# v projected for four heads at a time instead of two, in 512-column matmuls over four PSUM banks

## The chip, the cores and the metric

The kernel runs on one core of a Trainium2 chip. The metric is device time in microseconds (us) of one execution, with all transfers from and to device memory in it. TensorE (PE) multiplies, VectorE (DVE), ScalarE (ACT) and GpSimd (POOL) do the rest, and SyncE (SP) and POOL issue the transfers.

## What is computed

One encoder block on 512 tokens of width 2048, in float32. Cut to what matters:

```python
h = rmsnorm(x, norm_mix_g)
dq, dk, dv, nq, nk, nv = split(h @ w_in, 6)          # each 512 x 1024, 8 heads of 128
# differential attention, 8 heads: two softmaxes per head over all 512 keys
a = softmax(q1 @ k1.T / 8) - lam * softmax(q2 @ k2.T / 8)     # q, k with partial rotary
a_out = rmsnorm(a @ dv, subln_g) * (1 - lambda_init)
# neighbourhood attention, 8 heads: each token sees 8 x 16 neighbours on the 8 x 64 grid
n_out = softmax(nq @ nk.T / sqrt(128) + rel_bias + mask) @ nv
x = x + concat(a_out, n_out) @ w_out
x = x + square(relu(rmsnorm(x, norm_mlp_g) @ w_up)) @ w_down
y = rmsnorm(x, norm_final_g)
```

The two v, dv and nv, are 512 tokens x 1024 columns each, contracted over 2048 rows of w_in.

## The kernel before

Products are made in three matmuls: each float32 operand is split into a high part (`wh`, by a cast on ACT) and a remainder (`wl`, by a subtraction on DVE, of every third unit in the attention part on POOL), and high x high, high x low and low x high are summed in PSUM (`mm3`, L97 to L100). A unit of weights is 128 x 1024 float32, 512 KB, loaded and split by `load_unit` (L72 to L91). In the host's layout, a unit of w_dv or w_nv holds four k-tiles of 128 rows by 256 columns, that is two heads; there are four units to such a block. A unit of q or k weights holds eight k-tiles of 128 columns, one head.

PSUM has eight banks of 512 float32 columns per partition. Pool psA (four banks, `psa()`) serves the projections and later w_out, psB and psC (two banks each) the attention.

`v_banks` (L129) takes two banks of psA and cuts each into two halves of 256 columns, so that each of the four row tiles t of 128 tokens has a half. `v_mm` (L133) runs the matmuls of one unit for one row tile: the stationary operand is hT (x transposed, times the norm's gain, split into two parts), the moving one the 256 columns of the weights. `v_out` (L144) scales a row tile by the row norm r, once on ACT for the high part and once on DVE for the remainder.

The start (L150 to L193): the v block of heads 0 and 1 (`pv0`) is accumulated while x arrives. For each of four groups of four k-tiles, one unit of weights and the x tiles are loaded on SP's queue; ACT writes the high part of hT (L165), DVE the remainder (L166), and PE runs `v_mm`. The squares of x go through ACT (L178) and are added up on POOL (L179), a last addition is DVE's (L180), and a matmul with ones sums over partitions (L183). From that `rstd_of` (L102 to L112) makes r on DVE and ACT, and only then can `v_out` scale pv0.

The attention part (L406 to L420) goes through pairs of heads: `proj_v` for dv (but for the first pair, whose dv is pv0), `diff_head` of the first head, `proj_v` for nv, `na_head` of the first head, `diff_head` and `na_head` of the second; in the last pair both `diff_head` come first. `diff_head` (L274) projects q and k (`proj_T`, 48 matmuls of 512 columns into one bank of psA, L232), rotates and stacks them, and per row tile makes scores (L291, L292), softmax (L293 to L299) and transposes (L303); then probabilities times v, and a norm. `na_head` (L335) does the like for the neighbourhood. The last four halves of heads go to `mixT` on chip, the earlier ones by way of device memory, and w_out (L500 on) follows.

The order of the instructions on each engine is written ahead by a planner that weighs priorities and its own estimates of durations; at run time each engine takes its instructions in that order and waits by semaphores. The start has the highest priority, unit loads of the attention part are advanced (`ahead=3000`), everything else goes by program order. A buffer of a pool (a PSUM bank, say) can be taken again only when all readers of its former content are done. `ones_f` (L126) is a tile of ones, copied into `ones_r` (L201) later; `lam4` and `lprod` (L124, L222) hold the four lambda vectors and their products; `tb` (L339) is the bias table of a neighbourhood head.

Of the kernel before, what the change touches and what calls it, by code (L numbers as in the profile page):

```python
# [9 lines left out]
F32 = mybir.dt.float32  # L10
F32R = mybir.dt.float32r
# [10 lines left out]
NH = 8  # L22
# [13 lines left out]
def hymba_kernel(ctx: ExitStack, tc: tile.TileContext, x, x_t, norm_mix_g, w_dq, w_dk, w_dv, w_nq, w_nk, w_nv, lams,  # L36
# [20 lines left out]
    def psa():  # L57
        return psA.tile([P, 512], F32, name="pa", tag="pa")
# [38 lines left out]
    def mm3(ps, lh, ll, rh, rl, first, last):  # L97
        nc.tensor.matmul(out=ps, lhsT=lh, rhs=rh, start=first, stop=False)  # L98
        nc.tensor.matmul(out=ps, lhsT=lh, rhs=rl, start=False, stop=False)  # L99
        nc.tensor.matmul(out=ps, lhsT=ll, rhs=rh, start=False, stop=last)  # L100
# [16 lines left out]
    def hT_k(kt, hl):  # L117
        return hT[kt // 4][:, hl, kt % 4, :]
# [4 lines left out]
    nc.scalar.dma_start(out=gT, in_=norm_mix_g)  # L123
    lam4 = ap0.tile([P, 4 * 64], F32, name="lam4")  # L124
    rB = ap0.tile([P, SEQ], F32, name="rB")
    ones_f = ap0.tile([P, P], F32, name="ones_f")  # L126
    nc.vector.memset(ones_f, 1.0)

    def v_banks():  # L129
        b = [psa() for _ in range(2)]  # L130
        return [b[t // 2][:, (t % 2) * 256:(t % 2 + 1) * 256] for t in range(NT)]

    def v_mm(ps, t, u, wh, wl):  # L133

        ts = slice(t * P, (t + 1) * P)
        for k in range(4):
            kt = 4 * u + k
            first, last = kt == 0 and t % 2 == 0, kt == NK - 1
            lh, ll = hT_k(kt, 0)[:, ts], hT_k(kt, 1)[:, ts]
            for i, (a, b) in enumerate(((lh, wh), (lh, wl), (ll, wh))):  # L140
                nc.tensor.matmul(out=ps[t], lhsT=a, rhs=b[:, k, :], start=first and i == 0, stop=last and i == 2,  # L141
                                 skip_group_check=True)

# [7 lines left out]
    with tc.tile_pool(name="start", bufs=4) as sp, tc.high_priority(offset=20000):  # L151
        acc = sp.tile([P, 2 * SEQ], F32, name="acc", bufs=1)
        xs = []
        for u in range(4):

            wh, wl = load_unit(w_dv[0, u], 256, pool=sp, ahead=0, cuts=2 if u == 0 else 1)
            xt = sp.tile([P, 4, SEQ], F32, name="xt", tag="xt")
            n = 4 if u == 0 else 2
            for i in range(n):
                ks = slice(i * 4 // n, (i + 1) * 4 // n)  # L160
                nc.sync.dma_start(out=xt[:, ks, :], in_=x_t[u].rearrange("p (k s) -> p k s", k=4)[:, ks, :])
            xs.append(xt)
            for k in range(4):
                g, hi = gT[:, 4 * u + k:4 * u + k + 1], hT_k(4 * u + k, 0)
                nc.scalar.mul(hi, xt[:, k, :], g)  # L165
                nc.vector.scalar_tensor_tensor(out=hT_k(4 * u + k, 1), in0=xt[:, k, :], scalar=g, in1=hi.bitcast(F32),  # L166
                                               op0=ALU.mult, op1=ALU.subtract)
            for t in range(NT):
                v_mm(pv0, t, u, wh, wl)
        for u in range(4):  # L170
# [11 lines left out]
        for t in range(NT):  # L182
            nc.tensor.matmul(out=ssx[:, t:t + 1], lhsT=acc[:, t * P:(t + 1) * P], rhs=ones_f[:, 0:1],  # L183
                             start=True, stop=True)
# [11 lines left out]
    with es:  # L196
        ap1 = es.enter_context(tc.tile_pool(name="att1", bufs=1))
        ap2 = es.enter_context(tc.tile_pool(name="att2", bufs=2))

        ones_r = ap1.tile([P, P], F32R, name="ones_r")  # L200
        nc.vector.tensor_copy(out=ones_r, in_=ones_f)  # L201
        cos_sb = ap1.tile([P, SEQ], F32, name="cos_sb")
# [13 lines left out]
        with tc.issue_after(last_sq.ins):  # L216
            for r in range(GH):
                src = bass.AP(rel_bias.tensor, rel_bias.offset + 15 * 15 + 7 - r, [[TD * 15, NH], [-15, 16], [1, TRUN]])
                nc.gpsimd.dma_start(out=tbd[:, r::GH, :], in_=src)

        nc.sync.dma_start(out=lam4, in_=lams.broadcast_to([P, 256]))
        lprod = ap1.tile([P, 2, 64], F32, name="lprod")  # L222
        l4 = lam4.rearrange("p (i d) -> p i d", i=4)
# [18 lines left out]
        def proj_v(w, tag):  # L242

            ps = v_banks()
            for u in range(4):
                wh, wl = load_unit(w[u], 256, 3)
                for t in range(NT):
                    v_mm(ps, t, u, wh, wl)
            v = ap1.tile([P, 2, 4, 256], F32R, name=tag, tag=tag)
            v_out(v, ps)  # L250
            return v
# [22 lines left out]
        def diff_head(h, v):  # L274
# [30 lines left out]
            po = psb()  # L305
            vs = slice((h % 2) * HD, (h % 2 + 1) * HD)
            for k in range(4):
# [27 lines left out]
        def na_head(h, v):  # L335
# [56 lines left out]
            dst = {0: pj[:, 0::3], 1: pj[:, 0:2], 2: pj[:, 1:3], 3: pj[:, 2:4]}  # L392
            vs = slice((h % 2) * HD, (h % 2 + 1) * HD)
            for n, blk in enumerate((1, 3, 2, 0)):
# [10 lines left out]
        mixT = []  # L405
        for hp in range(NH // 2):  # L406
            if hp:
                dv = proj_v(w_dv[hp], "dv")
            else:
                dv = ap1.tile([P, 2, 4, 256], F32R, name="dv", tag="dv")  # L410
                v_out(dv, pv0)
            last = hp == NH // 2 - 1
            diff_head(2 * hp, dv)
            if last:
                diff_head(2 * hp + 1, dv)
            nv = proj_v(w_nv[hp], "nv")
            na_head(2 * hp, nv)
            if not last:
                diff_head(2 * hp + 1, dv)
            na_head(2 * hp + 1, nv)  # L420

# [517 lines left out]
```

## Time and profile before

| | us |
|---|---|
| median of 3 runs | 2129.21 (2128.66 to 2133.19) |
| profiled execution, its own time | 2128.14 |
| its span in the trace | 2126.0 |
| PE busy in the span | 2080.7 |
| DVE, ACT, POOL busy | 1527.0, 982.5, 282.6 |
| granted TensorE clock, mean share | 0.993 |

The durations of the trace come from the profiled execution. Busy time of PE is a sum of modelled durations in which neighbouring matmuls overlap, so a matmul's cost in a stream is the distance between starts, and not its own duration. In the chain of waits, "us, what x N" is a merged piece of N instructions.

### The profile page before, as it was taken

The numbers are of one execution on the slowest core, as the hardware profiler recorded it, in microseconds if no ns is written. First come the engines' busy times: TensorE is split into PE (matmuls) and PEld (weight loads), VectorE is DVE, ScalarE is ACT, GpSimd is POOL, SyncE is SP. The second block draws the span as 40 slices with busy tenths as digits, with TensorE's granted clock in tenths as the row PEclk, the third lists the DMA queues.
The fourth block names the chain that finished last, engine by engine and source line by source line (L and its number), as shares of the span: only waits on it lengthen the run. The fifth ranks groups of instructions, "written<-read, shape, count | busy, mean of one in ns | idle before, by whom it ended". The sixth has DMA issues, their size and how long they took to land.

```text
span 2126.0 us, 31142 instructions
## 1 busy us (share of the span) xinstructions
PE 2080.7 (98%) x12604; PEld 1853.7 (87%) x12604; DVE 1527.0 (72%) x1707; ACT 982.5 (46%) x1342; POOL 282.6 (13%) x271
## 2 busy tenths in 40 slices
PE   7999999999999999999999999999999999999996
PEld 6989989989888887999999999999888878788875
DVE  6656556556566345877777877778777788788788
ACT  5444444444445434444444444444554555445544
POOL 5221221221221000000000000000011111111110
PEclk8999999999999999999999999999999999999998
DMA  6322332332324642634334434335888798798873
GB/s 217 114 95 89 109 97 88 108 98 85 105 92 136 223 156 87 209 129 149 129 119 150 141 128 139 131 129 178 226 223 216 178 243 217 190 246 211 214 182 109
DMA packets 109552, 323.51 MB, mean 152 GB/s; under 512 B 11296, under 2 KB 27872, under 8 KB 109408
## 3 DMA queue, kind: packets, MB, share of 16 engines
q1 hardware_dynamic: 83040, 241.33, 34.0%
q0 software_dynamic: 25936, 79.65, 16.7%
q8 instruction: 99, 1.62, 0.3%
q10 hardware_dynamic: 432, 0.53, 0.1%
q14 instruction: 45, 0.37, 0.1%
HBM read 275.33 MB, written 30.25 MB: 144 GB/s over the span
## 4 chain that ended last, share of the span: by engine, by line
PE 81%; DVE 8%; DMA 5%; issue 2%; ACT 2%; POOL 0%; SPq 0%; ACTq 0%; DVEq 0%; POOLq 0%
PE pm L593 28%; PE x L776 13%; PE pa L141 8%; PE pa L98 7%; PE pa L99 7%; PE pa L100 7%; DMA b<-in_w_down 5%; DVE wl L95 3%; PE v L776 2%; PE pb L99 1%; PE pb L98 1%; PE pb L100 1%; DVE b L685 1%; PE pc L98 1%; PE pc L99 1%
## 5 line engine op out<-in xcount | busy, mean ns | idle before, releaser
L94 ACT CAST wh<-b 128x1024 fp32r<-128x1024 f32 x320 | 333.3, 1049 | 452.9 <-PE x L776 156.2
L776 PE MATMUL x<-wh,uT 128*128 128x512 f32 x1536 | 482.0, 392 | 8.7 <-DVE y L790 7.8
L95 DVE TENSOR_TENSOR wl<-b,wh 128x1024 fp32r<-128x1024 f32 x320 | 388.3, 1220 | 115.8 <-ACT wh L94 114.2
L776 PEld LDWEIGHTS x<-wh,uT 128*128 128x128 f32 x1536 | 288.8, 188 | 76.5 <-issue 4.5
L776 PE MATMUL x<-wl,uT 128*128 128x512 f32 x768 | 301.2, 392 | 0.9 <-DVE wl L95 0.9
L593 PE MATMUL pm<-s,wh 128*128 128x256 f32 x1536 | 280.2, 283 | 3.4 <-ACT p L598 2.3
L593 PE MATMUL pm<-a,wh 128*128 128x256 f32 x1536 | 267.3, 279 | 2.0 <-DVE c L611 1.4
L593 PEld LDWEIGHTS pm<-s,wh 128*128 128x128 f32 x1536 | 239.4, 192 | 4.0 <-ACT p L598 2.8
L593 PEld LDWEIGHTS pm<-a,wh 128*128 128x128 f32 x1536 | 232.8, 189 | 2.4 <-DVE c L611 1.6
L95 DVE TENSOR_TENSOR wl<-ts,wh 128x1024 fp32r<-128x1024 f32 x128 | 154.8, 1222 | 105.7 <-ACT wh L94 104.2
L89 ACT CAST wh<-raw 128x1024 fp32r<-128x1024 f32 (+1 forms) x129 | 134.5, 1043 | 200.3 <-PE pa L99 72.1
L593 PE MATMUL pm<-s,wl 128*128 128x256 f32 x768 | 217.9, 284 | 1.6 <-DVE wl L95 1.6
L94 ACT CAST wh<-ts 128x1024 fp32r<-128x1024 f32 x128 | 132.6, 1051 | 186.9 <-PE pm L593 165.7
L141 PE MATMUL pa<-wh,hT 128*128 128x256 f32 x1024 | 201.2, 291 | 14.1 <-DVE hT L166 7.9
L593 PE MATMUL pm<-a,wl 128*128 128x256 f32 x768 | 209.5, 278 | 0.0
L90 DVE TENSOR_TENSOR wl<-raw,wh 128x1024 fp32r<-128x1024 f32 (+1 forms) x98 | 121.0, 1235 | 117.7 <-ACT wh L89 116.1
L100 PE MATMUL pa<-hT,wl 128*128 128x512 f32 x512 | 201.3, 393 | 0.0
L99 PE MATMUL pa<-hT,wh 128*128 128x512 f32 x512 | 200.9, 392 | 0.0
L98 PE MATMUL pa<-hT,wh 128*128 128x512 f32 x512 | 200.7, 392 | 0.0
L141 PEld LDWEIGHTS pa<-wh,hT 128*128 128x128 f32 x1024 | 168.2, 197 | 18.9 <-DVE hT L166 9.3
L776 PEld LDWEIGHTS x<-wl,uT 128*128 128x128 f32 x768 | 144.5, 188 | 33.1 <-DVE wl L95 2.2
L593 PEld LDWEIGHTS pm<-s,wl 128*128 128x128 f32 x768 | 147.2, 192 | 2.0 <-DVE wl L95 2.0
(250 smaller groups left out, 3576.4 us busy)
## 6 DMA issues: line engine op xcount, KB each, us to landing
b<-in_w_down SPq DMA_DIRECT2D x130, 512.0 KB, 6.4
b<-in_w_up SPq DMA_DIRECT2D x128, 512.0 KB, 3.7
b<-in_w_down POOLq DMA_DIRECT2D x64, 512.0 KB, 10.2
raw<-in_w_out SPq DMA_DIRECT2D x32, 512.0 KB, 3.4
ud<-c POOLq DMA_DIRECT2D x32, 512.0 KB, 3.1
ur<-ud SPq DMA_DIRECT2D x32, 512.0 KB, 9.3
y<-st POOLq DMA_DIRECT2D x26, 512.0 KB, 11.1
raw<-in_w_dq SPq DMA_DIRECT2D x16, 512.0 KB, 3.4
```

The source lines that it names most:

```text
L89: nc.scalar.copy(out=wh[:, cs], in_=raw[:, cs])
L90: eng.tensor_sub(out=wl[:, cs], in0=raw[:, cs], in1=wh[:, cs].bitcast(F32))
L94: nc.scalar.copy(out=hi, in_=src)
L95: (eng or nc.vector).tensor_sub(out=lo, in0=src, in1=hi.bitcast(F32))
L98: nc.tensor.matmul(out=ps, lhsT=lh, rhs=rh, start=first, stop=False)
L99: nc.tensor.matmul(out=ps, lhsT=lh, rhs=rl, start=False, stop=False)
L100: nc.tensor.matmul(out=ps, lhsT=ll, rhs=rh, start=False, stop=last)
L141: nc.tensor.matmul(out=ps[t], lhsT=a, rhs=b[:, k, :], start=first and i == 0, stop=last and i == 2, skip_group_check=True)
L593: nc.tensor.matmul(out=ps, lhsT=a[:, k], rhs=s[k // 4][:, j, k % 4], start=first and k + i == 0, stop=last and k == 7 and i == 2, skip_gro ...
L685: nc.vector.tensor_add(out=a, in0=a, in1=b)
L776: m = nc.tensor.matmul(out=ps[:, b], lhsT=l, rhs=r[:, k], start=first and u + k + i == 0, stop=last and u == 1 and k == 1 and i == 2, skip ...
```

## The change

`v_banks` gives each row tile a bank of its own, `v_mm` runs matmuls of 512 columns (four heads) by `mm3`, over two k-tiles per unit, and the host lays w_dv and w_nv out in units of two k-tiles by 512 columns. A v block has eight units, and there are four blocks in place of eight. In the start, the unit loop is split in two halves of two k-tiles each. The attention loop goes over two groups of four heads. To make room for v tiles of twice the size, the ones are made once, from the identity, and the lambda vectors share the buffer of `tb`.

```diff
@@ -121,25 +121,19 @@
     ap0 = es.enter_context(tc.tile_pool(name="att0", bufs=1))
     gT = ap0.tile([P, NK], F32, name="gT")
     nc.scalar.dma_start(out=gT, in_=norm_mix_g)
-    lam4 = ap0.tile([P, 4 * 64], F32, name="lam4")
     rB = ap0.tile([P, SEQ], F32, name="rB")
-    ones_f = ap0.tile([P, P], F32, name="ones_f")
-    nc.vector.memset(ones_f, 1.0)
+    ones_r = ap0.tile([P, P], F32R, name="ones_r")
+    nc.vector.tensor_scalar(out=ones_r, in0=ident, scalar1=0.0, scalar2=1.0, op0=ALU.mult, op1=ALU.add)
 
     def v_banks():
-        b = [psa() for _ in range(2)]
-        return [b[t // 2][:, (t % 2) * 256:(t % 2 + 1) * 256] for t in range(NT)]
+        return [psa() for _ in range(NT)]
 
     def v_mm(ps, t, u, wh, wl):
 
         ts = slice(t * P, (t + 1) * P)
-        for k in range(4):
-            kt = 4 * u + k
-            first, last = kt == 0 and t % 2 == 0, kt == NK - 1
-            lh, ll = hT_k(kt, 0)[:, ts], hT_k(kt, 1)[:, ts]
-            for i, (a, b) in enumerate(((lh, wh), (lh, wl), (ll, wh))):
-                nc.tensor.matmul(out=ps[t], lhsT=a, rhs=b[:, k, :], start=first and i == 0, stop=last and i == 2,
-                                 skip_group_check=True)
+        for k in range(2):
+            kt = 2 * u + k
+            mm3(ps[t], hT_k(kt, 0)[:, ts], hT_k(kt, 1)[:, ts], wh[:, k, :], wl[:, k, :], kt == 0, kt == NK - 1)
 
     def v_out(v, ps):
         for t in range(NT):
@@ -152,21 +146,22 @@
         acc = sp.tile([P, 2 * SEQ], F32, name="acc", bufs=1)
         xs = []
         for u in range(4):
-
-            wh, wl = load_unit(w_dv[0, u], 256, pool=sp, ahead=0, cuts=2 if u == 0 else 1)
             xt = sp.tile([P, 4, SEQ], F32, name="xt", tag="xt")
-            n = 4 if u == 0 else 2
-            for i in range(n):
-                ks = slice(i * 4 // n, (i + 1) * 4 // n)
-                nc.sync.dma_start(out=xt[:, ks, :], in_=x_t[u].rearrange("p (k s) -> p k s", k=4)[:, ks, :])
             xs.append(xt)
-            for k in range(4):
-                g, hi = gT[:, 4 * u + k:4 * u + k + 1], hT_k(4 * u + k, 0)
-                nc.scalar.mul(hi, xt[:, k, :], g)
-                nc.vector.scalar_tensor_tensor(out=hT_k(4 * u + k, 1), in0=xt[:, k, :], scalar=g, in1=hi.bitcast(F32),
-                                               op0=ALU.mult, op1=ALU.subtract)
-            for t in range(NT):
-                v_mm(pv0, t, u, wh, wl)
+            for j in range(2):
+
+                n = 2 if u + j == 0 else 1
+                wh, wl = load_unit(w_dv[0, 2 * u + j], 512, pool=sp, ahead=0, cuts=n)
+                for i in range(n):
+                    ks = slice(2 * j + i * 2 // n, 2 * j + (i + 1) * 2 // n)
+                    nc.sync.dma_start(out=xt[:, ks, :], in_=x_t[u].rearrange("p (k s) -> p k s", k=4)[:, ks, :])
+                for k in (2 * j, 2 * j + 1):
+                    g, hi = gT[:, 4 * u + k:4 * u + k + 1], hT_k(4 * u + k, 0)
+                    nc.scalar.mul(hi, xt[:, k, :], g)
+                    nc.vector.scalar_tensor_tensor(out=hT_k(4 * u + k, 1), in0=xt[:, k, :], scalar=g,
+                                                   in1=hi.bitcast(F32), op0=ALU.mult, op1=ALU.subtract)
+                for t in range(NT):
+                    v_mm(pv0, t, 2 * u + j, wh, wl)
         for u in range(4):
             for i in range(2):
                 xh = xs[u][:, 2 * i:2 * i + 2, :]
@@ -180,7 +175,7 @@
         nc.vector.tensor_add(out=acc[:, :SEQ], in0=acc[:, :SEQ], in1=acc[:, SEQ:])
         ssx = psc()[:, :NT]
         for t in range(NT):
-            nc.tensor.matmul(out=ssx[:, t:t + 1], lhsT=acc[:, t * P:(t + 1) * P], rhs=ones_f[:, 0:1],
+            nc.tensor.matmul(out=ssx[:, t:t + 1], lhsT=acc[:, t * P:(t + 1) * P], rhs=ones_r[:, 0:1].bitcast(F32),
                              start=True, stop=True)
         r = rstd_of(ap0, ssx, DM, NT, "h")
         vx = keep.tile([P, NT], F32, name="vx")
@@ -197,8 +192,6 @@
         ap1 = es.enter_context(tc.tile_pool(name="att1", bufs=1))
         ap2 = es.enter_context(tc.tile_pool(name="att2", bufs=2))
 
-        ones_r = ap1.tile([P, P], F32R, name="ones_r")
-        nc.vector.tensor_copy(out=ones_r, in_=ones_f)
         cos_sb = ap1.tile([P, SEQ], F32, name="cos_sb")
         nc.scalar.dma_start(out=cos_sb, in_=cos_t)
         nc.vector.tensor_mul(out=cos_sb, in0=cos_sb, in1=rB)
@@ -218,8 +211,9 @@
                 src = bass.AP(rel_bias.tensor, rel_bias.offset + 15 * 15 + 7 - r, [[TD * 15, NH], [-15, 16], [1, TRUN]])
                 nc.gpsimd.dma_start(out=tbd[:, r::GH, :], in_=src)
 
+        lam = ap1.tile([P, 32 * 15], F32, name="lam", tag="tb")
+        lam4, lprod = lam[:, :256], lam[:, 256:384].rearrange("p (i d) -> p i d", i=2)
         nc.sync.dma_start(out=lam4, in_=lams.broadcast_to([P, 256]))
-        lprod = ap1.tile([P, 2, 64], F32, name="lprod")
         l4 = lam4.rearrange("p (i d) -> p i d", i=4)
         nc.vector.tensor_mul(out=lprod, in0=l4[:, 0::2, :], in1=l4[:, 1::2, :])
         lsum = ap1.tile([P, 2], F32, name="lsum")
@@ -242,11 +236,11 @@
         def proj_v(w, tag):
 
             ps = v_banks()
-            for u in range(4):
-                wh, wl = load_unit(w[u], 256, 3)
+            for u in range(8):
+                wh, wl = load_unit(w[u], 512, 3)
                 for t in range(NT):
                     v_mm(ps, t, u, wh, wl)
-            v = ap1.tile([P, 2, 4, 256], F32R, name=tag, tag=tag)
+            v = ap1.tile([P, 2, 4, 512], F32R, name=tag, tag=tag)
             v_out(v, ps)
             return v
 
@@ -303,7 +297,7 @@
                     nc.tensor.transpose(out=pt[:, k, :], in_=pr[:, 0, k * P:(k + 1) * P], identity=ident)
                 split(aTh[:, :, ts], aTl[:, :, ts], pt)
             po = psb()
-            vs = slice((h % 2) * HD, (h % 2 + 1) * HD)
+            vs = slice((h % 4) * HD, (h % 4 + 1) * HD)
             for k in range(4):
                 mm3(po, v[:, 0, k, vs], v[:, 1, k, vs], aTh[:, k, :], aTl[:, k, :], k == 0, k == 3)
             o = ap2.tile([P, SEQ], F32, name="o", tag="o")
@@ -390,7 +384,7 @@
             po = psb()
             pj = po.rearrange("p (j q) -> p j q", j=4)
             dst = {0: pj[:, 0::3], 1: pj[:, 0:2], 2: pj[:, 1:3], 3: pj[:, 2:4]}
-            vs = slice((h % 2) * HD, (h % 2 + 1) * HD)
+            vs = slice((h % 4) * HD, (h % 4 + 1) * HD)
             for n, blk in enumerate((1, 3, 2, 0)):
                 lh, ll = v[:, 0, blk, vs], v[:, 1, blk, vs]
                 for i, (a, b) in enumerate(((lh, pth), (lh, ptl), (ll, pth))):
@@ -403,21 +397,26 @@
             mixed(h, 1, o)
 
         mixT = []
-        for hp in range(NH // 2):
-            if hp:
-                dv = proj_v(w_dv[hp], "dv")
+        for hq in range(2):
+            if hq:
+                dv = proj_v(w_dv[1], "dv")
             else:
-                dv = ap1.tile([P, 2, 4, 256], F32R, name="dv", tag="dv")
+                dv = ap1.tile([P, 2, 4, 512], F32R, name="dv", tag="dv")
                 v_out(dv, pv0)
-            last = hp == NH // 2 - 1
-            diff_head(2 * hp, dv)
-            if last:
-                diff_head(2 * hp + 1, dv)
-            nv = proj_v(w_nv[hp], "nv")
-            na_head(2 * hp, nv)
-            if not last:
-                diff_head(2 * hp + 1, dv)
-            na_head(2 * hp + 1, nv)
+            h = 4 * hq
+            diff_head(h, dv)
+            nv = proj_v(w_nv[hq], "nv")
+            na_head(h, nv)
+            diff_head(h + 1, dv)
+            na_head(h + 1, nv)
+            diff_head(h + 2, dv)
+            if hq:
+                diff_head(h + 3, dv)
+                na_head(h + 2, nv)
+            else:
+                na_head(h + 2, nv)
+                diff_head(h + 3, dv)
+            na_head(h + 3, nv)
 
 
 
@@ -907,10 +906,10 @@
         "in_norm_mix_g": a("norm_mix_g", NK, P).T,
         "in_w_dq": units(wi[:, 0], 128),
         "in_w_dk": units(wi[:, 1], 128),
-        "in_w_dv": units(wi[:, 2], 256),
+        "in_w_dv": units(wi[:, 2], 512),
         "in_w_nq": units(wi[:, 3], 128),
         "in_w_nk": units(wi[:, 4], 128),
-        "in_w_nv": units(wi[:, 5], 256),
+        "in_w_nv": units(wi[:, 5], 512),
         "in_lams": np.concatenate([a(f"lambda_{n}", 1, 64) for n in ("q1", "k1", "q2", "k2")], axis=1),
         "in_diff_subln_g": a("diff_subln_g", HD, 1),
         "in_na_rel_bias": np.pad(a("na_rel_bias", NH, 15, 31).transpose(0, 2, 1), ((0, 0), (8, 8), (0, 0))),
```

## Rows read from the trace of the kernel before

**Rows 1.** The page: busy time, share of the span, instructions

```profile
PE 2080.7 (98%) x12604; PEld 1853.7 (87%) x12604; DVE 1527.0 (72%) x1707; ACT 982.5 (46%) x1342; POOL 282.6 (13%) x271
```

**Rows 2.** Busy time by stretch: start:end, length, engines, clock, DMA share, GB/s

```profile
0.00:47.00 47.00, 32.91 (x195) 30.91 (x196) 34.98 (x26) 25.69 (x33) 26.96 (x22) 0.85 0.68 220
...
100.00:200.00 100.00, 100.00 (x552) 86.73 (x551) 59.23 (x96) 43.36 (x76) 17.71 (x15) 1.00 0.29 92
```

**Rows 3.** PE's waits: us in total, times, longest

```profile
PE pa L141 <- DVE hT L166: 7.9, 6, 1.8
```

**Rows 4.** Busy time by stretch, within the start

```profile
29.40:36.20 6.80, 4.51 (x35) 4.09 (x34) 6.80 (x5) 0.22 (x1) 6.80 (x5) 1.00 0.03 6
36.20:39.60 3.40, 3.40 (x19) 3.40 (x18) 3.40 (x6) 0.00 (x0) 3.29 (x6) 0.51 0.84 253
```

**Rows 5.** The chain of waits in order of time: start, us, what

```profile
69.69 9.35 PE pa L141 x78
...
1494.33 32.94 PE x L776 x144
```

**Rows 6.** Timeline of PE: start, us, instruction, count

```profile
46.34 0.40 PE L98 MATMUL pa<-hT,wh 128*128 128x512 f32 x1
...
47.03 0.39 PE L98 MATMUL pa<-hT,wh 128*128 128x512 f32 x1
...
47.94 0.39 PE L99 MATMUL pa<-hT,wh 128*128 128x512 f32 x1
```

**Rows 7.** Line 141: count, duration ns, first and last start

```profile
L141 PE MATMUL pa<-wh,hT x1024: 274/283/581, 5.4 to 598.3; 128*128 128x256 f32 x171
```

**Rows 8.** Timeline of DVE in the start

```profile
14.38 11.21 DVE L166 SCALAR_TENSOR_TENSOR hT<-xt,gT,hT 128x512 fp32r<-128x512 f32 x4
25.51 1.21 DVE L90 TENSOR_TENSOR wl<-raw,wh 128x1024 fp32r<-128x1024 f32 x1
...
36.83 2.73 DVE L166 SCALAR_TENSOR_TENSOR hT<-xt,gT,hT 128x512 fp32r<-128x512 f32 x4
...
41.75 0.68 DVE L180 TENSOR_TENSOR acc<-acc 128x512 f32<-128x512 f32 x1
```

**Rows 9.** Timeline of POOL in the start

```profile
14.17 8.08 POOL L179 TENSOR_TENSOR acc<-acc,sqx 128x1024 f32<-128x1024 f32 x3 [0.81 <-ACT sqx L178]
```

**Rows 10.** Timeline, from the sum over partitions to the first scaling

```profile
54.74 0.95 PE L183 MATMUL pc<-ones_f,acc 128*128 128x1 f32 x8
...
55.73 0.16 DVE L105 TENSOR_SCALAR vh<-pc 128x4 f32<-128x4 f32 x1 [1.65 <-PE pc L183]
...
59.61 0.16 DVE L111 TENSOR_TENSOR rh<-rh,th 128x4 f32<-128x4 f32 x1
...
60.31 0.88 DVE L147 SCALAR_TENSOR_TENSOR dv<-pa,rh,dv 128x256 fp32r<-128x256 f32 x2
```

**Rows 11.** Groups by line, 0 to 1000 us: shapes, count, busy, mean ns

```profile
L255 ACT ACTIVATE qf<-pa 128x512 f32<-128x512 f32 x16 | 9.5, 593 | 0.0
...
L361 DVE TENSOR_TENSOR nf<-pa,rB 128x512 f32<-128x512 f32 x8 | 5.5, 688 | 7.6 <-PE pa L100 7.6
```

**Rows 12.** Timeline: the last v block's first scaling

```profile
595.26 0.47 ACT L146 ACTIVATE nv<-pa,rh 128x256 fp32r<-128x256 f32 x1 [1.05 <-PE pa L141]
```

**Rows 13.** Busy time by stretch: line 141 alone (PE, PEld), then all engines

```profile
545.00:600.00 55.00, 25.15 (x192) 24.40 (x192) 1.00 0.28 88
...
600.00:645.00 45.00, 45.00 (x201) 36.54 (x200) 35.84 (x47) 23.32 (x37) 9.45 (x6) 1.00 0.32 97
```

**Rows 14.** Timeline: probabilities done on DVE, and transposed on PE

```profile
563.08 0.75 DVE L299 SCALAR_TENSOR_TENSOR pr<-pr,l 128x512 f32<-128x512 f32 x1
...
568.36 0.60 PE L303 MATMUL pb<-ident,pr 128*128 128x128 f32 x4
...
639.76 0.75 DVE L299 SCALAR_TENSOR_TENSOR pr<-pr,l 128x512 f32<-128x512 f32 x1
...
645.01 0.60 PE L303 MATMUL pb<-ident,pr 128*128 128x128 f32 x4
```

## The prediction

> **What bounds the kernel now.** I read the page's first part first: PE is busy for 98% of the span [rows 1]. That is a share of modelled times, so the stages come next. From 47 us on, PE is busy in every microsecond of the attention part; the stretch of 100 us that is shown stands for all of them up to 800 us. Only the first 47 us have holes: 32.9 us of work [rows 2]. The list of PE's waits names their cause: DVE's writing of hT, 7.9 us in six waits, all in the start [rows 3]. The attention part is thus bound by how many matmul slots are issued, the start by DVE. So the change has to be priced in PE slots after the start, and in waits within it.
>
> **What a v matmul costs.** The chain of waits has PE running 78 v matmuls of 256 columns in 9.35 us, 0.1199 us each, and 144 of 512 columns in 32.94 us, 0.2288 us each [rows 5]. Nearer to the new form are the q projections of the attention part (same operands, 512 columns): four steps in 0.91 us, 0.2275 us each [rows 6]. I take 0.1198 and 0.228. The 1536 matmuls of 256 columns become 768 of 512: 1536 x 0.1198 = 184.0 us against 768 x 0.228 = 175.1 us. **Saved: 8.9 us** (9.3 by 0.2275, 8.3 by 0.2288). All of it would be on the path, as PE has no idle time behind the start.
>
> The Trainium skill (TensorE: Matmul & The Clock Gate, section Back-to-back issue gap) gives N / 2.4 + 2.5 ns for a warm matmul, which would make two of 256 columns only 2.5 ns dearer than one of 512. By that, the change would save an estimated 1.9 us here. The rows say 2 x 119.8 - 228 = 11.6 ns per pair, and they are this kernel's own stream of weight loads and matmuls, so they decide.
>
> **The start.** Before, v of heads 0 and 1 is made there; after, v of heads 0 to 3. The v matmuls begin at 5.4 us [rows 7] and the q projection behind them at 46.34 us [rows 6]: 46.3 us for 192 x 0.1198 = 23.0 us of work, 23.3 us lost. 5.4 of these lie ahead of the first matmul, whose operands arrive in the same pieces as before; the other 17.9 are waits and slow clock. Why: a k-tile of x needs one hT operation on DVE, 0.68 us when DVE is alone (four in 2.73 us), but 2.80 us while POOL adds squares (four in 11.21 us) [rows 8], and POOL does that back to back, three in 8.08 us [rows 9]. PE's work on a k-tile is 12 x 0.12 = 1.4 us, so PE waits.
>
> After, PE's work on a k-tile is 12 x 0.228 = 2.74 us. A unit of two k-tiles needs three DVE operations: two hT and a wl of 1.21 us alone [rows 8]. In the POOL stretch (seven adds of some 2.7 us, about 20 us) that is 3 x 2.80 = 8.4 us against 5.5 us on PE: PE loses 2.9 us per unit, on 20 / 8.4 = 2.4 units, 7 us. Behind it DVE needs 2.6 us per unit and is ahead for good. With 3 us for the slow clock that such waits bring (the granted clock is 0.51, the 1.2 GHz level, for 3.40 us behind one of them [rows 4]) the loss is 5.4 + 10 = 15.4 us instead of 23.3. **Saved: 7.9 us**, between 0 (all 17.9 stay) and 14 (4 of them stay). The v block then ends at 15.4 + 192 x 0.228 = 59.2 us.
>
> The start loads four more units of weights, 2 MB. The DMA engines stand nearly idle from 29.4 to 36.2 us (share 0.03 [rows 4]), with everything of the start landed, so I price that at nothing; if it does come late, the 14 shrinks first. The four more splits on ACT and DVE in the start are taken from later; DVE's are in the sum above.
>
> **What the four banks cost.** psA has four banks and all projections use them. Before, pv0 held two, and the first q projection ran in a third while pv0 waited for the row norms. After, pv0 holds all four until v_out has scaled them, and v_out needs r. So nothing can run on PE between the last v matmul and the first v_out, except the sum over partitions that r needs. Before, that sum sat on PE at 54.74 us although DVE had finished its input at 42.4 us [rows 8, 10]: the written order has it late, 8.4 us behind the last v matmul. If it comes behind the last v matmul again, the wait is the rest of the chain: DVE's first step at 55.73 us to its last at 59.61 + 0.16 us [rows 10], then scaling one bank, 0.59 us on ACT and 0.69 us on DVE at 512 columns [rows 11]. With the hand-overs, 55.7 to about 61.2: 5.5 us. A wait of that length takes the clock down; by the 3.40 us at 0.51 above, 1.7 us more. **Lost: 7.2 us**, between 0 (the chain is done under the v matmuls) and 10 (twice the slow clock and a queued split ahead of v_out on ACT).
>
> The Trainium skill (Perfetto Trace Analysis, section Matmuls) asks that independent groups rotate through different PSUM banks, so that the evacuation of one runs beside the next group's matmuls; here there is no bank left to rotate to. What that is worth is the 7.2 us above.
>
> The other three v blocks also hold all four banks, but no norm is awaited. There v_out begins before the block ends: the last block's first scaling stands at 595.26 us [rows 12], its last v matmul at 598.3 us [rows 7]. With one bank per row tile, bank 0 ends 18 matmuls ahead of the block, 4.1 us, and needs 1.3 us of scaling plus a queue. Priced at nothing; its cover is those 4.1 us, and without them each block would cost 1.3 us.
>
> **The small edits.** ones_r made from ident instead of a memset and a later copy, lam in the buffer of tb: a fraction of a microsecond on DVE in places where PE has other work; nothing. v_out has half as many operations, on engines that have slack behind the start; nothing. One unit's subtraction moves from POOL to DVE; nothing.
>
> **The order of the heads.** Blocks of v work fill PE while attention waits for DVE and ACT. After, they are twice as long and half as many; none lies behind diff_head 7, where now 192 v matmuls stand between 545 and 600 us [rows 13]. What covers the loss: attention's PE work is late by order and not by data. DVE finished the probabilities at 563.08 + 0.75 us and PE transposed them at 568.36 us; later at 640.51 and 645.01 us [rows 14]: 4.5 us of slack at each of these steps, eight of them in the last two diff heads. And in 600 to 645 us, with no v matmul at all, PE is full while DVE is at 35.84 of 45 us [rows 13]. I price it at nothing.
>
> **Sum.** 8.9 + 7.9 - 7.2 = 9.6 us off the profiled execution's own 2128.14 us (span 2126.0): 2118.5 us. The median of the runs lies 1.07 us above the profiled one: **2119.6 us**.
>
> **Rivals.**
> - The norm chain ends under the longer v block and the wait at the four banks falls away. For it: the v block ends some 13 us later and the squares hardly do. Against it: the order is written ahead and put the sum late. 2119.6 - 7.2 = 2112.4 us.
> - The start saves nothing: the added splits keep DVE locked to POOL as long as before in proportion. 2119.6 + 7.9 = 2127.5 us, no change that can be measured.
> - A pair of matmuls saves 2.5 ns only, by the rule above; rows 5 and 6 contradict. 7.0 us less saved: 2126.6 us.
> - On the other side: attention starves. Without a v block behind diff_head 7, PE reaches the end of its projections 192 x 0.1198 = 23.0 us earlier against attention and then waits for DVE; it cannot go to w_out, since that needs four psA banks and two may be held by k and q of the last heads. Price: up to 23.0 us at the last pair, 2142.6 us. It decides where the eight slacks of up to 4.5 us (36 us at most, some 25 if they are smaller) are used up before the cover is. For it: DVE is at 80% in 600 to 645 us [rows 13]; against it, PE never waited there.
>
> **How the numbers follow.** Forecast 0.42 (own range 2114 to 2126: bounds of the start and of the wait), no wait at the banks 0.23, no gain in the start 0.12, page rule 0.03, starved attention 0.17 (2128 to 2143), anything else 0.03. The range takes the first two, the small ones between, and the cheaper half of the starved case: 2107 to 2137. A change of 0.2%, 4.3 us, is about what a measurement of this kernel can tell: faster is below 2124.9. Faster 0.63: nine tenths of the forecast, all of the second case, little else. Same 0.19: the third and fourth case and the forecast's upper end. Slower 0.18: the starved case.
>
> **What would show it.** In the profile of the changed kernel: 768 v matmuls, 0.228 us apart; the first q projection at about 65 us, and ahead of it one PE wait of about 5 us that ends with DVE's or ACT's v; the granted clock down behind it; the v block itself ended near 59 us; behind 70 us no PE wait of over a microsecond until the w_out part. A v block that ends past 65 us makes the start term wrong; PE waits for DVE or ACT between 500 and 720 us make the order of the heads the cause, and the forecast wrong with it.

## The result: slower, and the profile after

The changed kernel took **2152.8 us** in the median (2151.79 to 2159.51, four runs) against 2128.93 us of the kernel before on the same chip (2127.86 to 2133.19): ratio **1.0119, 95% interval [1.0105, 1.0132]**. The forecast was 2119.6 us, and at most 2137 us. The profiled execution of the changed kernel is its slowest, 2159.51 us (span 2157.7), 6.7 us above the median.

The page of the changed kernel; the row stands against [rows 1]:

```profile
PE 2087.9 (97%) x11836; PEld 1819.6 (84%) x11836; DVE 1533.0 (71%) x1691; ACT 980.9 (45%) x1326; POOL 284.5 (13%) x270
```

768 matmuls are gone, as they should be. The busy time of PE hardly tells of it, since it is modelled and grows where the clock is low (a matmul of 512 columns counts 0.39 us at the higher clock and 0.63 us at the lower). So the stages come next. Busy time by stretch of the changed kernel: start:end, length, PE, PEld, DVE, ACT, POOL, granted clock, DMA share, GB/s.

```profile
60.00:80.00 20.00, 14.07 (x59) 11.46 (x59) 6.91 (x20) 6.45 (x9) 7.18 (x8) 0.83 0.25 71
100.00:200.00 100.00, 100.00 (x464) 82.98 (x463) 53.21 (x79) 41.68 (x67) 21.71 (x17) 1.00 0.31 96
640.00:680.00 40.00, 29.68 (x107) 22.03 (x106) 29.96 (x32) 16.94 (x22) 10.90 (x6) 0.87 0.47 139
680.00:720.00 40.00, 32.48 (x152) 25.57 (x152) 30.56 (x59) 22.20 (x46) 2.51 (x3) 0.87 0.17 56
```

The same 80 us of the kernel before:

```profile
640.00:680.00 40.00, 40.00 (x190) 33.12 (x189) 28.86 (x41) 23.44 (x35) 9.65 (x6) 1.00 0.48 151
680.00:720.00 40.00, 40.00 (x199) 33.55 (x198) 17.15 (x33) 17.66 (x35) 0.00 (x0) 1.00 0.48 163
```

From 640 to 720 us PE is idle for 17.8 of 80 us, where it had been full, and its clock falls to 0.87: these stretches mix the 1.2 and the 2.4 GHz level. Up to the last matmul of the q and k projections the changed kernel was ahead: that one starts at 640.3 us, before at 647.3. From there to the first matmul of w_up it takes 228.1 us against 194.4. So 7.0 us are gained and 33.7 lost, in all 26.7 us at that point. Behind it the two traces differ by another 5.0 us (1289.4 against 1284.4); that stretch, which no edit touches, takes between 1280 and 1291 us in the ten traces of this document, so these 5.0 us are not put down to the change.

What PE waits for there: the five longest on the list of PE's waits of the changed kernel from 70 to 720 us (us in total, times, longest).

```profile
PE pa L98 <- DVE nf L348: 5.9, 1, 5.9
PE pc L98 <- DVE lg L374: 4.3, 2, 3.3
PE pa L98 <- DVE dv L141: 2.5, 1, 2.5
PE pa L98 <- DVE nf L355: 2.2, 1, 2.2
PE pb L311 <- ACT sqh L94: 1.8, 1, 1.8
```

All but the third lie in the last heads and are for DVE or ACT, which the prediction named as the sign against itself. The longest is that of w_out's first matmul (646.58 us): it needs a bank of psA that still holds the q of a neighbourhood head, and DVE comes to that (`nf`) late. What DVE is late with shows in its timeline. Chosen rows of the last diff head's rotary in the changed kernel (start, us, engine, line):

```profile
634.12 0.73 DVE L251 STREAM_SHUFFLE sh<-qf 128x512 f32<-128x512 f32 x1
...
643.01 0.75 DVE L316 SCALAR_TENSOR_TENSOR o<-o,gsub,rs 128x512 f32<-128x512 f32 x1
643.87 0.69 DVE L255 TENSOR_TENSOR qr<-qf,sh 128x512 f32<-128x512 f32 x1
...
645.09 0.72 DVE L251 STREAM_SHUFFLE sh<-qf 128x512 f32<-128x512 f32 x1
645.70 0.73 DVE L348 SCALAR_TENSOR_TENSOR nf<-pa,rB 128x384 f32<-128x384 f32 x2
...
654.24 0.68 DVE L255 TENSOR_TENSOR qr<-qf,sh 128x512 f32<-128x512 f32 x1
...
658.07 2.75 DVE L265 TENSOR_TENSOR kx<-qr,kx 64x512 fp32r<-64x512 f32 x1
```

q of this head left PSUM at 579.38 us (L249) and then lay for 55 us. Its `sh` is one buffer, under a tag that the norm of the head before uses for its `sq`, and its `qr` shares one with that norm's `rs`. The norm ends at 643.01 + 0.75 us, and only then can `qr` be written; k's rotary follows, and the head's first scores come at 663.89 us. So a diff head cannot finish its rotary until the one before has ended its norm. In the changed kernel `qr` of q follows the end of the norm before it within 1.4 us at heads 2, 3, 6 and 7, those with no v block between them and the diff head before; in the kernel before only at head 7, for the same reason. The theory for the experiments is thus (theory A in what was expected of them): **two single buffers chain the diff heads, and the change pushes this chain past its cover.** Rivals: (B) w_out lacks psA banks at the end, whatever the chain; (C) the heads stand in the wrong order; (D) DVE has too much work; (E) r's longer chain through `lam` at the start costs the time.

### The profile page after: what moved, and what is told of

Read it like the earlier page. It is cut to its first block, busy times and chain, and to the rows that moved or that the text cites. A ratio compares the mean times of both kernels' runs of the same rounds, so it can differ in the third digit from the quotient of the medians.

```text
span 2157.7 us, 29587 instructions
## 1 busy us (share of the span) xinstructions
PE 2087.9 (97%) x11836; PEld 1819.6 (84%) x11836; DVE 1533.0 (71%) x1691; ACT 980.9 (45%) x1326; POOL 284.5 (13%) x270
## 4 chain that ended last, share of the span: by engine, by line
PE 79%; DVE 9%; DMA 7%; issue 3%; ACT 1%; POOL 0%; SPq 0%; ACTq 0%; DVEq 0%; POOLq 0%
PE pm L592 28%; PE x L775 15%; PE pa L99 9%; PE pa L98 9%; PE pa L100 9%; DMA b<-in_w_down 5%; PE v L775 2%; DVE wl L95 2%; PE pb L99 1%; PE pb L100 1%; PE pb L98 1%; PE pc L98 1%; PE pc L100 1%; PE pc L99 1%; PE pc L286 1%
## 5 line engine op out<-in xcount | busy, mean ns | idle before, releaser
L90 DVE TENSOR_TENSOR wl<-raw,wh 128x1024 fp32r<-128x1024 f32 (+1 forms) x99 | 127.8, 1294 | 140.6 <-ACT wh L89 140.2
L592 PEld LDWEIGHTS pm<-a,wl 128*128 128x128 f32 x768 | 143.3, 189 | 0.0
L98 PEld LDWEIGHTS pa<-hT,wh 128*128 128x128 f32 x512 | 96.6, 189 | 22.5 <-DVE dv L141 3.3
```

The costliest lines, as they stand in the source:

```text
L90: eng.tensor_sub(out=wl[:, cs], in0=raw[:, cs], in1=wh[:, cs].bitcast(F32))
L592: nc.tensor.matmul(out=ps, lhsT=a[:, k], rhs=s[k // 4][:, j, k % 4], start=first and k + i == 0, stop=last and k == 7 and i == 2, skip_gro ...
```

## The experiments

Each run stands beside runs of the kernel before on the same chip, and ratios are to that.

**The norm in other buffers (e1).** The change, with the norm's two temporaries under tags that the rotary doesn't use:

```diff
-            sq = ap1.tile([P, SEQ], F32, name="sq", tag="sh")
+            sq = ap2.tile([P, 2, SEQ], F32, name="sq", tag="pr")[:, 0, :]
...
-            r = ap1.tile([P, SEQ], F32, name="rs", tag="qr")
+            r = ap1.tile([P, SEQ], F32, name="rs", tag="sqh")
```

> Changed kernel (2152.8 us), but the norm of a diff head no longer uses the single buffers sh and qr of the rotary: its square lies in a buffer of pr, its root in that of sqh. Theory A (the next head's rotary waits for the norm of the head before, so diff heads without a v block between them follow each other at 69 to 77 us, PE runs out of projections at 640 us and starves): the chain shortens, 20 to 34 us less, 2119 to 2133 us, and PE's idle time between 640 and 720 us (17.8 us now) goes below 8. Rival B (w_out lacks psA banks at the end): nothing changes, 2148 to 2157 us. Rival D (DVE's throughput sets the pace of attention): nothing changes either.

Measured: 2121.87 us, ratio 0.9975 [0.9961, 0.9988]. The whole loss is gone, with the same banks, the same order of heads in the program and the same work on DVE: B and D fall. E falls too, since r's chain still goes through `lam` and the first q still comes at 69.10 us. The planner writes the order of the instructions anew for each kernel; what the two buffers cost as waits and what by the order written around them, these runs do not tell apart. DVE's timeline of this kernel, the norm of head 6 and the rotary of head 7:

```profile
582.74 0.68 DVE L255 TENSOR_TENSOR qr<-qf,sh 128x512 f32<-128x512 f32 x1
...
592.57 0.68 DVE L255 TENSOR_TENSOR qr<-qf,sh 128x512 f32<-128x512 f32 x1
...
636.21 0.75 DVE L316 SCALAR_TENSOR_TENSOR o<-o,gsub,rs 128x512 f32<-128x512 f32 x1
```

The rotary now ends 43 us ahead of the norm. And in this kernel's 640 to 720 us (columns as above) PE is idle for 0.45 us only, at the full clock:

```profile
640.00:720.00 80.00, 79.55 (x386) 66.04 (x385) 51.76 (x81) 43.37 (x79) 12.03 (x10) 1.00 0.54 181
```

**lam loaded early (e2).** The change, with `lam4` and its products made at the very start, in rB's still unused buffer:

```diff
+    lam4, lprod = rB[:, :256], rB[:, 256:384].rearrange("p (i d) -> p i d", i=2)
+    nc.scalar.dma_start(out=lam4, in_=lams.broadcast_to([P, 256]))
...
-        lam = ap1.tile([P, 32 * 15], F32, name="lam", tag="tb")
-        lam4, lprod = lam[:, :256], lam[:, 256:384].rearrange("p (i d) -> p i d", i=2)
-        nc.sync.dma_start(out=lam4, in_=lams.broadcast_to([P, 256]))
...
```

> Changed kernel, but the four lambda vectors are loaded at the very start into rB (free until r is known) and their products made there, instead of in the buffer of tb behind the start. In the changed kernel DVE waits 2.1 us for that load in the midst of the steps towards r, while PE stands still. If PE's time up to the last projection before diff_head 5 passes on to the end (theory A says so, the chain of the last three diff heads starts there): 2 to 3 us less, 2150 us. If the end is set by DVE's total work (rival D): no change.

Measured: 2152.12 us, ratio 1.0115 [1.0088, 1.0142], as the change. The load was in r's chain. DVE's timeline, the first and the last step of r; the changed kernel first, then this one:

```profile
61.96 0.16 DVE L105 TENSOR_SCALAR vh<-pc 128x4 f32<-128x4 f32 x1 [14.59 <-PE pc L178]
...
66.42 0.29 DVE L218 TENSOR_TENSOR lam<-lam 128x128 f32<-128x128 f32 x1 [2.13 <-DMA lam<-in_lams]
...
67.14 0.16 DVE L111 TENSOR_TENSOR rh<-rh,th 128x4 f32<-128x4 f32 x1
```

```profile
64.74 0.16 DVE L105 TENSOR_SCALAR vh<-pc 128x4 f32<-128x4 f32 x1 [15.47 <-PE pc L184]
...
67.49 0.16 DVE L111 TENSOR_TENSOR rh<-rh,th 128x4 f32<-128x4 f32 x1
```

The chain fell from 5.3 to 2.9 us, but the v block's last matmul came 2.8 us later (63.5 against 60.7 us), and r came no sooner. The whole block is shifted: with the load of `lam` added beside it, x arrives later for ACT's first hT (7.42 us instead of 4.66), and PE's first matmul waits for that. The first rows of PE, the changed kernel and then this one:

```profile
5.44 0.80 PE L98 MATMUL pa<-wh,hT 128*128 128x512 f32 x1 [5.44 <-ACT hT L160]
```

```profile
8.20 0.79 PE L98 MATMUL pa<-wh,hT 128*128 128x512 f32 x1 [8.20 <-ACT hT L166]
```

The first q begins at 69.22 us, against 68.86. So the run took nothing off PE's start, and what an earlier start would have been worth it does not show.

**diff 5 ahead of the nv block (e3).** The change, with the second group in the order diff 4, diff 5, nv, na 4, diff 6, na 5, diff 7, na 6, na 7:

```diff
             diff_head(h, dv)
+            if hq:
+                diff_head(h + 1, dv)
             nv = proj_v(w_nv[hq], "nv")
             na_head(h, nv)
-            diff_head(h + 1, dv)
+            diff_head(h + 1 + hq, dv)
             na_head(h + 1, nv)
-            diff_head(h + 2, dv)
             if hq:
                 diff_head(h + 3, dv)
                 na_head(h + 2, nv)
             else:
+                diff_head(h + 2, dv)
                 na_head(h + 2, nv)
```

> Changed kernel with another order of heads in the second group: diff 4, diff 5, v of the neighbourhood heads, na 4, diff 6, na 5, diff 7, na 6, na 7. Theory A: the chain of diff heads 5 to 7 begins up to 44 us earlier and the v block lies beside it; na heads then come later than diff heads, so part of it is lost again: 10 to 30 us less, 2123 to 2143 us. Rival B (banks at the end): within 5 us of 2152.8. Rival D: DVE's work is spread somewhat more evenly, 0 to 10 us less.

Measured: 2125.83 us, ratio 0.9987 [0.9976, 0.9998]. So the order cures it too (C), but mostly by starting the chain sooner and not by making it faster. First scores of diff heads 4 to 7, in us, from the traces:

| kernel | 4 | 5 | 6 | 7 |
|---|---|---|---|---|
| before | 395.8 | 475.1 | 555.8 | 616.9 |
| after | 419.5 | 518.6 | 587.3 | 663.9 |
| norm in other buffers | 416.9 | 515.0 | 574.4 | 607.1 |
| diff 5 ahead of nv | 419.4 | 486.3 | 556.0 | 620.2 |

With the shared buffers, two diff heads stand at least 61 us apart in every kernel (76.6 in the change's last pair); in other buffers 32.7 are possible, and 27.1 in the run after this one. The new order starts the last links 32 us sooner, and the last of them takes 64.2 us instead of 76.6. The chain is the limit, and the order decides whether it reaches past the projections.

**The norm in other buffers, in the kernel before (e7).** The same edit on the old kernel.

> The kernel before (2128.9 us) with the same change of the norm's buffers as in e1. Theory A: there the projections of the next diff head end behind the norm of the one before (but for head 7), since a v block of two heads lies between, so the buffers hold nothing up: within 0.2%, 2124.7 to 2133.2 us. If the buffers limit attention everywhere, it gets faster by more than that, 5 to 10 us.

Measured: 2127.88 us, ratio 1.0002 [0.999, 1.0014]. Head 7's first scores come at 582.6 instead of 616.9 us, and the time doesn't move: before, the chain was there and covered. So the gain of the first experiment is the repair of what the change broke.

**Halves (e4).** The first experiment's kernel, with each 512-column v matmul made as two of 256 into halves of the same bank; everything else, the four banks too, stays.

```diff
-            mm3(ps[t], hT_k(kt, 0)[:, ts], hT_k(kt, 1)[:, ts], wh[:, k, :], wl[:, k, :], kt == 0, kt == NK - 1)
+            for c in range(2):
+                cs = slice(256 * c, 256 * c + 256)
...
+                    nc.tensor.matmul(out=ps[t][:, cs], lhsT=p, rhs=q[:, k, cs], start=kt == 0 and c == 0 and i == 0,
+                                     stop=kt == NK - 1 and i == 2, skip_group_check=True)
```

> The kernel of e1 (norm buffers apart, 2121.9 us, PE without a wait over 1 us from 69 us to the end of w_out), but each v matmul of 512 columns is made as two of 256 columns into the halves of the same bank. Everything else, the four banks and the order of the heads too, stays. This prices the columns alone, as PE sets the pace in e1. By the distance of starts in the changed kernel (0.231 us, against 2 x 0.1197 us): 768 x 8.4 ns = 6.5 us more, 2128.4 us. By my forecast's 0.228 us: 8.9 us more, 2130.8 us. By the page rule: 1.9 us more, 2123.8 us.

Measured: 2134.07 us, ratio 1.0035 [1.0022, 1.0048], 0.60% or 12.8 us above the first experiment's 0.9975, more than any of the three prices. In the traces, neighbouring v matmuls behind the start are 0.1207 us apart in the mean at 256 columns, and 0.2308 us at 512 in the first experiment: 10.6 ns a pair, 6.1 us on the 576 pairs of the three blocks. At the first matmul of w_up the lag is 8.8 us; some 1.9 us of it are PE's idle time from 100 to 640 us (2.2 us against 0.3). The remaining 4 us lie behind w_up's first matmul or between executions and are not shown to be the columns'. The column term is real. The rule of the Trainium skill that was weighed against it (TensorE: Matmul & The Clock Gate, Back-to-back issue gap) would give 2.5 ns a pair. The section gives it as the gap of a single matmul by itself; in these streams, with a weight load for every matmul, 10.6 ns were measured instead.

**Spare banks for the first q and k (e8).** The first experiment's kernel, with the first diff head's q projected into a bank of psB and its k into one of psC, while pv0 holds psA:

```diff
-        def proj_T(w):
+        def proj_T(w, ps=None):
...
-            ps = psa()
+            ps = psa() if ps is None else ps
...
-            pq = proj_T(w_dq[h])
+            pq = proj_T(w_dq[h], psb() if h == 0 else None)
...
-            pk = proj_T(w_dk[h])
+            pk = proj_T(w_dk[h], psc() if h == 0 else None)
```

> The kernel of e1, but the q and k projections of the first diff head go into a bank of psB and one of psC, which are free then, and not into psA. Theory: the wait of PE from the last v matmul of the start (61.0 us) to the first q matmul (69.1 us) comes from the four banks that wait for the row norm, so it goes, with the slow clock behind it: 7 to 9 us less, 2113 to 2115 us. Rival: the wait is not the banks' (the projections need something else of the norm chain, or the planner puts them behind it anyway): no change, 2120 to 2124 us.

Measured: 2114.88 us, ratio 0.9946 [0.9932, 0.9959], 0.29% or 6.2 us below the first experiment; 8.6 us at the first matmul of w_up. The timeline of PE behind the first v block, the changed kernel and then this one:

```profile
60.75 0.39 PE L100 MATMUL pa<-wh,hT 128*128 128x512 f32 x1
60.98 0.95 PE L178 MATMUL pc<-ones_r,acc 128*128 128x1 f32 x8
...
67.85 1.12 PE L187 MATMUL pb<-ident,rB 128*128 128x128 f32 x4 [5.93 <-DVE nlam L224]
...
68.86 0.79 PE L98 MATMUL pa<-hT,wh 128*128 128x512 f32 x1
...
70.31 0.63 PE L98 MATMUL pa<-hT,wh 128*128 128x512 f32 x1
70.73 0.63 PE L99 MATMUL pa<-hT,wh 128*128 128x512 f32 x1
...
72.60 0.39 PE L98 MATMUL pa<-hT,wh 128*128 128x512 f32 x1
```

```profile
60.50 0.39 PE L100 MATMUL pa<-wh,hT 128*128 128x512 f32 x1
60.73 0.95 PE L178 MATMUL pc<-ones_r,acc 128*128 128x1 f32 x8
61.54 0.48 PE L98 MATMUL pc<-hT,wh 128*128 128x512 f32 x1
```

The wait at the four banks is there, 5.93 us, and behind it the q matmuls stand 0.43 us apart (the 1.2 GHz level) until 72.4 us, and 0.23 us from then on. With spare banks q begins as soon as the sum over partitions is done, 0.23 us apart nearly from the first.

**Squares on DVE (e9).** That kernel, with six of the seven additions of squares in the start on DVE instead of POOL:

```diff
-                last_sq = nc.gpsimd.tensor_add(out=a3, in0=a3, in1=sq)
+                last_sq = (nc.gpsimd if u + i == 4 else nc.vector).tensor_add(out=a3, in0=a3, in1=sq)
```

> The kernel of e8, but six of the seven additions of squares in the start run on DVE and not on POOL (the last stays, as POOL's transfers are ordered behind it). Theory: POOL's additions hold DVE up (2.8 us per hT operation beside them, 0.68 us alone), which makes PE wait in the start; without them DVE needs some 8 us for the six but 15 us less for its own, and the v block of the start ends at 54 to 57 us in place of 61: 4 to 7 us less than e8. Rival: the slow operations in the start are not POOL's doing (transfers, ACT): 0 to 4 us more than e8, for the added work on DVE.

Measured: **2107.4 us**, ratio 0.9919 [0.9906, 0.9931], the fastest of all. DVE's timeline in the start, the changed kernel (its start is the same as that of the run before) and then this one:

```profile
21.33 5.72 DVE L161 SCALAR_TENSOR_TENSOR hT<-xt,gT,hT 128x512 fp32r<-128x512 f32 x2
...
28.11 5.71 DVE L161 SCALAR_TENSOR_TENSOR hT<-xt,gT,hT 128x512 fp32r<-128x512 f32 x2
```

```profile
14.34 1.41 DVE L161 SCALAR_TENSOR_TENSOR hT<-xt,gT,hT 128x512 fp32r<-128x512 f32 x2
15.67 1.22 DVE L174 TENSOR_TENSOR acc<-acc,sqx 128x1024 f32<-128x1024 f32 x1
```

An hT operation takes 2.86 us beside POOL's additions and 0.71 us without. The addition itself costs DVE 1.22 us. The v block's last matmul starts at 51.71 us, sooner than the 54 to 57 expected, and r's first step comes at 52.92 us instead of 61.96.

**Squares on DVE, in the kernel before (e10).** The same one-line edit.

> The kernel before, with six of its seven additions of squares in the start moved from POOL to DVE, the edit that took 7.5 us off the four-head version with the spare banks. Theory: the start of the kernel before is held by the same thing, DVE's hT operations of 2.8 us beside POOL's additions. Then hT takes about 0.7 us, the six PE waits of 7.9 us in all are gone, the slow clock with them, and the first q projection starts 5 to 9 us earlier than 46.3 us; the median falls by 5 to 9 us, ratio 0.996 to 0.998. Rival: with 256 columns a k-tile of PE work is only 1.4 us, so the start is then held by the arrival of x or by DVE's own work (two hT, half a wl and an addition are about 2.6 us per k-tile pair), and what was a wait for a slow hT becomes a wait for a late one: first q projection at 44 us or later, ratio 0.999 to 1.001.

Measured: 2116.65 us, ratio 0.9949 [0.9936, 0.9962], 10.8 us less, more than the theory gave. DVE's hT takes 0.71 us here too:

```profile
14.10 1.41 DVE L166 SCALAR_TENSOR_TENSOR hT<-xt,gT,hT 128x512 fp32r<-128x512 f32 x2
```

PE's waits in the start are two, for ACT's first hT (7.1 us, 5.1 of them ahead of the first matmul). The first v block's last matmul starts at 33.45 us instead of 46.22, with q matmuls already among its own, and the first matmul of w_up comes 10.0 us sooner. This sets the last experiment in its place: most of its gain isn't the change's. What four heads at a time are worth, once repaired (other buffers for the norm, spare banks for the first q and k), is 0.9919 / 0.9949 = 0.9970 with the squares on DVE in both: 6.4 us, 0.3%. The two were timed at different times, each against the kernel before, and by their intervals together it may be 2.5 to 10 us; at the first matmul of w_up the two traces stand 11.4 us apart.

## Why the prediction was wrong

**The failed step is "The order of the heads", "I price it at nothing".** Measured from the last projection to w_up, it cost 33.7 us. With the norm in other buffers the same stretch takes 197.1 us instead of 228.1, so 30.9 us of these are the chain's, as much as the first experiment took off the median; the other 2.8 us are work that the earlier end of the projections leaves behind it (some 950 matmuls against 923). The step took the slack at two transposes (4.5 us each [rows 14]) for a reserve that adds up over eight such places. But that slack says how long a finished result waits for PE, whose order is written ahead; it doesn't say how soon the next head can start. That is set by the buffers, and no row on the list of PE's waits shows it as long as other work covers it. The place to look at was a tag used by two steps of neighbouring heads, and the time for which q lay finished. The kernel before had shown it: q of head 7 left PSUM at 556.77 us, and its `qr` came 49 us later, right behind the norm of head 6. From its timelines of ACT and DVE:

```profile
556.77 0.59 ACT L255 ACTIVATE qf<-pa 128x512 f32<-128x512 f32 x1
...
605.14 0.74 DVE L322 SCALAR_TENSOR_TENSOR o<-o,gsub,rs 128x512 f32<-128x512 f32 x1
605.99 0.69 DVE L261 TENSOR_TENSOR qr<-qf,sh 128x512 f32<-128x512 f32 x1
```

With the norm in other buffers (e7) this `qr` starts at 561.02 us.

The rival on the other side, "attention starves", was right in kind, down to w_out's want of a psA bank, and short in price (2142.6 us at most). It counted the missing 23.0 us of v work at the end. What it left out is that the same work didn't vanish but moved ahead of the chain. The start now makes dv for four heads, so the first q comes 22.5 us later (68.86 against 46.34 us [rows 6]); the nv block of heads 6 and 7 now stands ahead of diff 5, some 23 us more. Head 5's first scores thus come 43.5 us later than before, and the chain behind them can't be made shorter by a free PE. The slow clock adds to it: 0.87 over 80 us is at most 0.13 x 80 = 10.4 us, beside the 17.8 us idle.

**The column term** was right: 8.9 us forecast, 7.9 measured. Between neighbouring v matmuls behind the start, the mean distance is 0.1208 us before and 0.2313 us after: 768 x (0.2416 - 0.2313) = 7.9 us. The forecast's 0.1198 and 0.228 came from single stretches, one of them of four steps [rows 6]; means over the whole attention part lie a little higher for both widths, and the q and k matmuls of 512 columns, 0.2306 us apart after, cost nearly as much as those of v.

**The start** was nearly right. The v block ended at 61.0 us (forecast 59.2), the loss in it is 61.0 - 192 x 0.2313 = 16.6 us instead of 46.3 - 192 x 0.1208 = 23.1: 6.5 us saved, 7.9 forecast. The mechanism held: hT 2.86 us beside POOL, 0.68 us alone behind it. POOL's stretch was longer than the 20 us taken, 12.2 to 36.0 us in the trace, with pauses for the squares and one `wl` of 2.87 us of POOL's own.

**The four banks** were priced at 7.2 us and are worth 6.2 by the ratio, 8.6 at w_up. q began at 68.86 us, not 65: 1.8 us from the later v block, and 2.1 us of the **small edit "lam in the buffer of tb"**, priced at nothing. Its load is issued at 61.99 us, and DVE stands 2.13 us before it, with r's chain queued behind. It was wrong as a step. What its removal alone would win stays open, since in the second experiment the added load put off the first matmul by more than that.

**v_out of the later blocks** was hidden but once: 2.5 us of the dv block of heads 4 to 7 (the wait on L141's dv above). Its tile is a single buffer that the first group's diff heads must leave first.

Put together, with the chain repaired, the forecast's sum nearly holds by its measured terms: 7.9 + 6.5 - 8.6 = 5.8 us at the first matmul of w_up, where the first experiment is 4.6 us ahead of the kernel before (837.1 against 841.7 us); the last 1.2 us are not accounted for. The forecast's 9.6 us were too high by a little in each of the three.

## What to carry to other kernels

Before filler work is moved or merged, trace the chain from one iteration to the next through each single buffer (a tag used by two steps), and compare its length with the work that lies between; slack where results wait for an engine with a fixed order says nothing about it. An accumulation that takes every bank of a pool and needs a late scalar is a barrier: give the next projection a bank elsewhere. Where DVE's two-input operations stand at four times their time alone, look at POOL first: in both kernels here, an addition that cost POOL 2.7 us [rows 9] and DVE 1.22 was better on DVE, even though DVE was what PE waited for.

## What the runs showed of the hardware

DVE's operation with two SBUF inputs (hT) took 2.86 us beside POOL's additions and 0.71 us without. The Trainium skill (SBUF — State Buffer, Who interferes with whom) says that the port pair that the two engines share is an exclusive lock, and the traces agree. It holds the other way too: with the squares on DVE, one `wl` of POOL's own took 9.39 us and ended only after DVE had gone idle at 36.0 us, where such operations in the kernel before take 2.44 us in the mean; the one addition left on POOL, with DVE idle, took 2.39 us. POOL's timeline in that run:

```profile
28.87 9.39 POOL L90 TENSOR_TENSOR wl<-raw,wh 128x1024 fp32r<-128x1024 f32 x1 [27.56 <-ACT wh L89]
38.24 2.39 POOL L174 TENSOR_TENSOR acc<-acc,sqx 128x1024 f32<-128x1024 f32 x1
```

That this was worth 10.8 us to the kernel before, whose PE waits named only 7.9 us [rows 3], was not expected. Slow clock behind such waits [rows 4] would come on top of them, but how the 10.8 us divide no run shows.
